# Input projection of a hybrid encoder layer: ten pairs of weight tiles as two-by-two block products in a stage of their own

## The chip, the cores and the metric

The kernel runs on one core of a Trainium2 chip. That core has five engines with instruction queues of their own: TensorE (PE in the profile; its weight loads are PEld), VectorE (DVE), ScalarE (ACT), GpSimd (POOL) and SyncE (SP), whose queue issues nearly all DMA transfers here. The metric is the device time of one launch in microseconds (us).

## The reference

One step of a one-layer encoder over 1152 tokens: 1024 of a prompt and 8 x 16 sample tokens with caches. In float32:

```python
h = rmsnorm(x, g_pre_mix)
qa, ka, va, qb, kb, vb, ga, gb = project(h, w_in)        # h @ w_in, 1024 -> 4352 columns
oa = band attention of qa over ka, va                    # 8 heads, 2 kv heads, own chunk + 2, sinks, T5 bias
ob = band attention of qb over kb, vb                    # 8 heads, own chunk + 8, relative bias
merged = sigmoid(ga) * (oa @ w_oa) + sigmoid(gb) * (ob @ w_ob)
x = x + rmsnorm(merged @ w_out, g_post_mix)
f, conv_new = conv_ffn(rmsnorm(x, g_pre_ffn), ...)       # up and gate, causal conv, gelu, down
x = x + rmsnorm(f, g_post_ffn)
```

Beside x it returns the last rows of ka, va, kb and vb and the state of the convolution.

## The kernel before

**Number format.** Each float32 operand of a large product is split into a high and a low part (`hi`, rounded to the type fp32r, and `lo`, the rest), and three matmuls (hi x hi, hi x lo, lo x hi) stand for one. `mm3` (L117 to L123) does this for the projections.

**Layout.** Activations lie transposed: channels on the 128 partitions, tokens along the rows. The 4352 columns of `w_in` are 34 tiles of 128. Tiles 0 to 3 are the queries of branch A (two heads each), 4 and 5 its keys and values, 6 to 9, 10 to 13 and 14 to 17 queries, keys and values of B, 18 to 33 the two gates.

**Stages.** (1) Nine blocks of 128 tokens are loaded, normalised, transposed on TensorE (L131) and split into `hT`, three groups of 384 tokens (L133, L134). (2) Projections and attention together. (3) Output projections `w_oa`, `w_ob` with the gates (L579 to L615). (4) `w_out`, norms, transposes (to L740). (5) The FFN's up and gate products (L774), with the convolution between. (6) The down product (L1039) and the final norm.

**Projections.** A tile's weights come in one transfer of 512 KB and are split by ACT (L105) and POOL (L108). Its product is three pieces, one for each group, of 24 matmuls of 128x384 into one PSUM bank (`piece`). ACT evacuates a piece: queries, keys and values into `raw` (L214), gates into `gt`, stored to `gate_dr` in DRAM (L276, L277). When a tile of queries, keys or values is complete, `q_done`, `k_done` or `v_done` split its rows, send new cache rows out and transpose values.

**Attention.** There are eight units: 0 to 3 for A (two heads each), 4 to 7 for B. A unit has six steps, four over 256 prompt tokens each and two over four samples each. A step computes scores (L344), adds bias and takes the minimum on DVE (L347), exponentiates on ACT (L352), scales (L367); the next step transposes the result on TensorE (L384, copied out at L386 and L388) and multiplies with the values (L399, L401), and the output goes to `o_dr` in DRAM (L402). Pieces of projection are laid between these items in quarters of six matmuls (`spread`): unit u carries the projections of unit u + 1 and `gates_per_unit` pieces of gates. Nine gate pieces remain after the last unit; one stands before its last transposes, one before its last `values`, seven behind.

**Stage 3's inputs.** The eight rows of `o_dr` are read into two buffers (`or`, pool `wx`, L588) and split (L589 on DVE, L590 on DVE or POOL) into `oT`. The first output tile needs units 0 to 3 for its first branch and 4 to 7 for its second.

**Bias tables.** Two small tables are replicated over 128 rows in DRAM by 16 transfers (L96); each unit reads its bias from them (L308, L414). This stands after the first two pieces of ka and va.

**Order.** The framework's scheduler orders each engine's instructions by the order of the program and by an estimate of when each is ready, so that a piece of projection may go ahead of a step that is not ready. On the chip each queue is then worked off in that order; waits are semaphores. Memory of a finished pool is given to the next pool at the same place, tile by tile.

**The block form.** Stages 5 and 6 already use a two-by-two block product with seven block products. In stage 5 the left factors are sums of quarters of two weight tiles, the right ones (b11, b21, t3, t2, t1, b22, t4) sums of quarters of the activations, each 512 channels by 576 tokens. A product (`product`, L770 to L775) is 24 matmuls of 128x288. `head_away` computes the two products that need only the first half of the activations and stores them, `tail` does the other five.

## Time and profile before

| | us |
|---|---|
| median of 3 runs | 1684.24 (1683.12 to 1687.8) |
| the profiled execution, its own time | 1683.2 |
| its span, from the first to the last instruction | 1681.1 |
| PE busy | 1631.1 |
| DVE busy | 964.7 |
| ACT busy | 668.7 |
| POOL busy | 315.1 |

A row of the profile names a line of the kernel, an engine, an operation and its tiles (written <- read, numbers left out in the page). `idle ... <- X` tells how long the engine stood still before these instructions and what released it. Matmuls are pipelined, so that the duration of one (0.34 us) is longer than the distance to the next (0.17 us). In windows, busy time counts each engine by itself. The profiled execution is one of several; its sums are compared with its own time.

### The profile page before, as it was taken

What the parts mean: (1) busy time and instruction counts of PE and PEld (TensorE: products, weight loads), DVE (VectorE), ACT (ScalarE), POOL (GpSimd) and SP (SyncE); (2) the same over time, 40 slices, a digit from 0 to 9 for tenths busy, and PEclk for the clock granted to TensorE, in tenths of its full rate; (3) what the DMA queues carried; (4) which work ended last, traced back from release to release, by engine and by line L of the source; (5) the groups of instructions that cost most, each with busy time, mean ns of one, the idle gap of its engine ahead of it and who ended that gap; (6) DMA issues with size and microseconds to landing.
All of it is one profiled execution on the core that took longest, in us unless ns stands there. A gap on an engine that the chain in (4) does not pass through costs nothing. (4 is left out here: it accounts for less than half of the span.)

```text
span 1681.1 us, 26782 instructions
## 1 busy us (share of the span) xinstructions
PE 1631.1 (97%) x10599; PEld 1505.6 (90%) x10599; DVE 964.7 (57%) x1815; ACT 668.7 (40%) x1309; POOL 315.1 (19%) x349
## 2 busy tenths in 40 slices
PE   5999999999999999999989899999999998999997
PEld 4999889899899999988889899999999997888886
DVE  6134442444443345444479676666666665965986
ACT  5244443333333322242354344444444444534342
POOL 2322122122221134420001211111111110000003
PEclk9999999999999999999999999999999999999999
DMA  5522323222222255452245322122212218043023
GB/s 190 177 87 80 110 82 95 71 70 69 77 85 70 70 174 178 137 179 100 85 134 159 111 82 79 68 76 80 72 62 79 80 55 315 36 182 138 1 90 136
DMA packets 84846, 177.37 MB, mean 106 GB/s; under 512 B 20536, under 2 KB 45672, under 8 KB 84720
## 3 DMA queue, kind: packets, MB, share of 16 engines
q1 hardware_dynamic: 84720, 175.65, 31.3%
q8 instruction: 83, 1.36, 0.4%
q14 instruction: 43, 0.35, 0.1%
HBM read 131.78 MB, written 48.56 MB: 107 GB/s over the span
## 5 line engine op out<-in xcount | busy, mean ns | idle before, releaser
L774 PE MATMUL x<-xot,s 128*128 128x288 f32 x1152 | 158.0, 295 | 1.8 <-DVE s L668 1.5
L774 PEld LDWEIGHTS x<-xot,s 128*128 128x128 f32 x1152 | 154.9, 188 | 2.2 <-DVE s L668 1.7
L1039 PE MATMUL x<-wbp,zap 128*128 128x512 f32 x576 | 135.3, 389 | 0.0
L1039 PEld LDWEIGHTS x<-wbp,zap 128*128 128x128 f32 x576 | 108.1, 188 | 22.4
L352 ACT ACTIVATE p<-p,m 128x256 f32<-128x256 f32 (+4 forms) x128 | 75.2, 589 | 105.3 <-DVE m L347 105.2
L1039 PE MATMUL p<-wbp,zap 128*128 128x512 f32 x432 | 102.0, 392 | 0.0
L667 ACT ACTIVATE s<-uw 128x512 fp32r<-128x512 f32 x96 | 60.0, 626 | 96.6 <-issue 43.2
L1039 PEld LDWEIGHTS p<-wbp,zap 128*128 128x128 f32 x432 | 82.0, 190 | 17.2
L870 DVE SCALAR_TENSOR_TENSOR wk<-w,cw,wk 128x128 f32<-128x128 f32 (+2 forms) x144 | 84.0, 619 | 7.8 <-ACT wk L868 7.0
L774 PE MATMUL x<-xob,s 128*128 128x288 f32 x576 | 82.6, 299 | 4.2 <-ACT wk L868 3.0
L668 DVE TENSOR_TENSOR s<-uw,s 128x512 fp32r<-128x512 f32 x96 | 67.3, 702 | 32.2 <-ACT s L667 32.2
L774 PEld LDWEIGHTS x<-xob,s 128*128 128x128 f32 x576 | 79.6, 191 | 4.7 <-ACT wk L868 3.2
L774 PE MATMUL z<-xot,s 128*128 128x288 f32 x576 | 80.7, 295 | 0.0
L774 PE MATMUL z<-xot,a 128*128 128x288 f32 x576 | 80.7, 295 | 0.0
L668 DVE TENSOR_TENSOR a<-uw,a 128x512 fp32r<-128x512 f32 x62 | 42.8, 691 | 63.5 <-ACT a L667 62.3
L774 PEld LDWEIGHTS z<-xot,s 128*128 128x128 f32 x576 | 78.1, 188 | 0.0
L774 PEld LDWEIGHTS z<-xot,a 128*128 128x128 f32 x576 | 78.1, 188 | 0.0
L774 PE MATMUL x<-xob,a 128*128 128x288 f32 x456 | 63.9, 295 | 0.0
L774 PE MATMUL y<-xob,a 128*128 128x288 f32 x456 | 63.9, 295 | 0.0
L774 PEld LDWEIGHTS x<-xob,a 128*128 128x128 f32 x456 | 61.8, 188 | 0.0
L774 PEld LDWEIGHTS y<-xob,a 128*128 128x128 f32 x456 | 61.8, 188 | 0.0
L347 DVE CUSTOM_DVE_ANT_0 p<-s,bt 128x320 f32<-128x320 f32 (+4 forms) x64 | 29.0, 489 | 56.2 <-PE s L344 55.5
(1216 smaller groups left out, 4123.0 us busy)
## 6 DMA issues: line engine op xcount, KB each, us to landing
uw<-in_w_upg SPq DMA_DIRECT2D x53, 512.0 KB, 4.4
gate_dr<-gt SPq DMA_DIRECT2D x48, 192.0 KB, 2.2
gg<-gate_dr SPq DMA_DIRECT2D x16, 576.0 KB, 3.9
z_dr<-wk SPq DMA_DIRECT2D x24, 256.0 KB, 2.1
z_dr<-wk SPq DMA_DIRECT2D x24, 224.0 KB, 1.9
xt<-in_x SPq DMA_DIRECT2D x9, 512.0 KB, 6.9
or<-o_dr SPq DMA_DIRECT2D x8, 576.0 KB, 4.3
xr<-in_x SPq DMA_DIRECT2D x9, 512.0 KB, 3.7
```

Source lines behind the costliest of these rows:

```text
L347: nc.vector.tensor_tensor_reduce(p[h][:, c * cw:(c + 1) * cw], ps[:, h, 0:cw], un.bt[h][:, w - n + c * cw:w - n + (c + 1) * cw], 1.0, leas ...
L352: nc.scalar.activation(p[h][:, 0:n], p[h][:, 0:n], AF.Exp, bias=least[h], scale=-1.0, accum_out=st.d[:, h, i:i + 1])
L667: nc.scalar.activation(sp[:, 0], src, AF.Copy)
L668: nc.vector.tensor_tensor(sp[:, 1], src, fr(sp[:, 0]), op=ALU.subtract)
L774: nc.tensor.matmul(ps[c], w[:, i, k], xo[name][:, j, c, k], start=first and k + i + j == 0, stop=last and k == 3 and i == 1, skip_group_ch ...
L870: nc.vector.scalar_tensor_tensor(out, src(t), cw[:, f, t:t + 1], out, op0=ALU.mult, op1=ALU.add)
L1039: nc.tensor.matmul(ps, z[:, i, k, c], w[:, j, k], start=first and n == 0, stop=last and n == 2, skip_group_check=True)
```

## The change

Twenty of the 34 tiles, as the ten pairs `pairs`, are computed in a stage ahead of attention, in the block form of stage 5; the other 14 stay as pieces between the attention steps. All 34 have their rows in DRAM (`in_dr`), and attention reads what it needs (`fetch`).

- The transposes now fill four quarters in float32 (`qa`, `qb`) by ACT; the splits (`parts_of`) run on 288 tokens at a time, the first two behind the third and the fifth block. The split activations are in `xk`, which takes the memory of `hT` and stays through attention.
- Five pairs go through `head_away`: two products, one part stored to `a1_dr`, one finished quarter to `in_dr`. Two of these stand ahead of the bias tables, three behind. Then each pair has its `tail`.
- `fetch(0)` stands before the first unit, `fetch(u + 1)` before the fourth step of unit u. It loads rows of 1152 tokens, scales queries on ACT, and goes on as `q_done`, `k_done`, `v_done` do.
- 42 pieces remain. `pieces_per_unit` lays 39 into the units, three remain after the last one.
- Memory for stages 3 to 6 (`r1`, `r2`) is opened only after attention. `left_factors`, `product` and `banks` now serve both block stages.

```diff
--- before
+++ after
+    in_dr = [dram.tile([P, T], F32, name=f"in_dr{i}") for i in range(34)]
+    gate_dr = in_dr[18:]
...
+    def left_factors(raw, ahead, name, part):
+        a11, a12, a21, a22 = raw[:, 0, 0:4], raw[:, 0, 4:8], raw[:, 1, 0:4], raw[:, 1, 4:8]
+        if not ahead:
+            yield part(a11, f"a11_{name}")
+            yield part(a12, f"a12_{name}")
+        nc.vector.tensor_tensor(a11, a11, a21, op=ALU.subtract)
+        yield part(a11, f"s3_{name}")
+        nc.vector.tensor_tensor(a11, a22, a11, op=ALU.subtract)
+        yield part(a11, f"s2_{name}")
+        nc.vector.tensor_tensor(a21, a21, a22, op=ALU.add)
+        yield part(a21, f"s1_{name}")
+        nc.vector.tensor_tensor(a12, a12, a11, op=ALU.subtract)
+        yield part(a12, f"s4_{name}")
+        yield part(a22, f"a22_{name}")
+
...
+    xkp = xk_stack.enter_context(tc.tile_pool(name="xk", bufs=1, reuse_waits="tile"))
+    xk = [xkp.tile([P, 2, 4, T], F32R, name=f"xk{i}") for i in range(2)]
...
+        pairs = [(4, 5), (0, 1), (2, 3), (10, 14)] + [(18 + n, 26 + n) for n in range(6)]
+        NA = 5
+        a1_dr = [dram.tile([P, 2, CW], F32, name=f"a1_dr{f}") for f in range(NA)]
+        rf = {}
...
+        def parts_of(t, src, c):
+
+            hi = t[:, 0, :, chunk(c)]
+            nc.scalar.activation(hi, src[:, :, chunk(c)], AF.Copy)
+            nc.vector.tensor_tensor(t[:, 1, :, chunk(c)], src[:, :, chunk(c)], fr(hi), op=ALU.subtract)
...
+        for i, name in enumerate(("b11", "b12")):
+            rf[name] = xk[0][:, :, :, i * 2 * CW:(i + 1) * 2 * CW]
+        for i, name in enumerate(("b21", "b22")):
+            rf[name] = xk[1][:, :, :, i * 2 * CW:(i + 1) * 2 * CW]
...
+        def head_away(f):
+
+            raw = wraws.pop(f, None) or weights(f, 1)
+            xb = banks(psx, f"ixh{f}")
+            product(xb, split_left(raw[:, 0, 0:4], f"ih11_{f}"), of(rf["b11"]), True, True)
+            a = copy_out(xb, two_chunks(f"iah{f}"))
+            nc.sync.dma_start(a1_dr[f][:], a[:])
+            yb = banks(psz, f"iyh{f}")
+            product(yb, split_left(raw[:, 0, 4:8], f"ih12_{f}"), of(rf["b21"]), True, True)
+            store(plus(yb, a, two_chunks(f"ich{f}")), pairs[f][0], 0)
...
-                sq = xp.tile([P, D], F32, name=f"sq{tb}", tag="sq", bufs=2)
+                if tb in (1, 3):
+                    wraws[tb // 2] = weights(tb // 2, 1)
                 st = xp.tile([P, 2], F32, name=f"st{tb}", tag="st")
-                nc.scalar.activation(sq[:], xt[:], AF.Square, accum_out=st[:, 0:1])
+                xn = xp.tile([P, D], F32, name=f"xn{tb}", tag="xn")
+                nc.scalar.activation(xn[:], xt[:], AF.Square, accum_out=st[:, 0:1])
                 rstd_of(st[:, 0:1], st[:, 1:2])
-                xn = xp.tile([P, D], F32, name=f"xn{tb}", tag="xn")
                 nc.vector.scalar_tensor_tensor(xn[:], xt[:], st[:, 1:2], gp[:], op0=ALU.mult, op1=ALU.mult)
-                transpose_to(pst, xn, hT, tb)
-                if tb in (2, 5):
-                    name = ("ka", "va")[tb // 3]
-                    early[name] = weight_tile(w_in[4 + tb // 3], name)
-
+                for q, quads in enumerate(((b11, b12), (b21, b22))):
+                    pt = psz.tile([P, 4, P], F32, name=f"tp{tb}_{q}", tag="ps")
+                    for k in range(4):
+                        nc.tensor.transpose(pt[:, k], xn[:, (4 * q + k) * P:(4 * q + k + 1) * P], ident[:])
+                    done = 0
+                    while done < P:
+                        h, t = divmod(tb * P + done, 2 * CW)
+                        n = min(P - done, 2 * CW - t)
+                        nc.scalar.activation(quads[h][:, :, t:t + n], pt[:, :, done:done + n], AF.Copy)
+                        done += n
+                if tb in (2, 4):
+                    for name, b in (("b11", b11), ("b21", b21)):
+                        parts_of(rf[name], b, tb // 2 - 1)
+
+            for f in range(2):
+                head_away(f)
+
...
+            replicate(tab_b, ext_b, eb, EXT_B)
...
+            replicate(tab_a, ext_a, ea, EXT_A)
+
+        tpool = [ph.enter_context(tc.tile_pool(name=f"t{i}", bufs=1, reuse_waits="tile")) for i in (3, 2, 1)]
...
+        def right_factors():
+
+            for n, pool in zip(("t3", "t2", "t1"), tpool):
+                rf[n] = pool.tile([P, 2, 4, 2 * CW], F32R, name=n)
+            for c in range(2):
+                cc = chunk(c)
+                parts_of(rf["b12"], b12, c)
+                nc.vector.tensor_tensor(b11[:, :, cc], b12[:, :, cc], b11[:, :, cc], op=ALU.subtract)
+                nc.vector.tensor_tensor(b12[:, :, cc], b22[:, :, cc], b12[:, :, cc], op=ALU.subtract)
+                parts_of(rf["t3"], b12, c)
+            yield
+            for c in range(2):
+                cc = chunk(c)
+                nc.vector.tensor_tensor(b12[:, :, cc], b22[:, :, cc], b11[:, :, cc], op=ALU.subtract)
+                parts_of(rf["t2"], b12, c)
+            yield
+            for c in range(2):
+                parts_of(rf["t1"], b11, c)
+            yield
+            for c in range(2):
+                cc = chunk(c)
+                parts_of(rf["b22"], b22, c)
+                nc.vector.tensor_tensor(b21[:, :, cc], b21[:, :, cc], b12[:, :, cc], op=ALU.subtract)
+            rf["t4"] = rqa.tile([P, 2, 4, 2 * CW], F32R, name="t4", tag="q")
+            for c in range(2):
+                parts_of(rf["t4"], b21, c)
+            yield
+
...
+        def head_back(f):
+            a = two_chunks(f"ia{f}")
+            nc.sync.dma_start(a[:], a1_dr[f][:])
+            return left_factors(weights(f), True, f"i{f}", split_left), banks(psx, f"ix{f}"), a
+
+        def tail(f, ops, xb, a, forms):
+            def take(name):
+                t = two_chunks(f"{name}{f}")
+                return copy_out(xb, t) if a is None else plus(xb, a, t)
+
+            t0, t1 = pairs[f]
+            zb = banks(psz, f"iz{f}")
+            product(zb, next(ops), of(rf["t3"]), True, False)
+            next(forms, None)
+            product(xb, next(ops), of(rf["t2"]), a is not None, False)
+            next(forms, None)
+            u2 = take("iu")
+            product(xb, next(ops), of(rf["t1"]), False, False)
+            next(forms, None)
+            u4 = take("iv")
+            store(plus(zb, u4), t1, 1)
+            product(xb, next(ops), of(rf["b22"]), False, True)
+            store(take("iw"), t0, 1)
+            product(zb, next(ops), of(rf["t4"]), False, True)
+            store(plus(zb, u2), t1, 0)
+
+        forms = right_factors()
+        for f in range(2, NA):
+            head_away(f)
+            if f == 2:
+                next(forms)
+        for f in range(len(pairs)):
+            tail(f, *(head_back(f) if f < NA else head(f)), forms)
...
+        def dense_pieces(col):
 
             box = {}
 
             def run(g):
                 if g == 0:
...
+                    box["w"] = weight_tile(w_in[col], f"w{col}")
+                w, c = box["w"], slice(g * GW, (g + 1) * GW)
+                ps = psd.tile([P, GW], F32, name=f"d{col}_{g}", tag="d")
+                for k in range(0, KD, 2):
+                    mm3(ps[:], w, [xk[k // 4][:, j, :, c] for j in range(2)], k % 4, 2, start=k == 0,
+                        stop=k == KD - 2, wk0=k)
+                    if k < KD - 2:
+                        yield
+                gt = gst.tile([P, GW], F32, name=f"gt{col}_{g}", tag="gt")
+                nc.scalar.activation(gt[:], ps[:], AF.Copy)
+                nc.sync.dma_start(in_dr[col][:, c], gt[:])
...
+        def rows(col, name, done, scale=None):
+
+            raw = rawp.tile([P, T], F32, name=f"{name}raw", tag="raw")
+            nc.sync.dma_start(raw[:], in_dr[col][:])
+            if scale is not None:
+                nc.scalar.activation(raw[:], raw[:], AF.Copy, scale=scale)
+            done(raw)
...
+        def fetch(u):
+
             un = units[u]
             if u < 4:
-                out = []
                 if u == 0:
-                    out += projection_pieces(4, "ka", 1.0, k_done(shared_a, "a", ka_new, 896))
-                    out += projection_pieces(5, "va", 1.0, v_done(shared_a, "a", va_new, 896))
-                return out + projection_pieces(u, f"q{u}", -0.125, q_done(un, u))
-            p = u - 4
-            return (projection_pieces(10 + p, f"k{u}", 1.0, k_done(un, f"{u}", kb_new[p], 512))
-                    + projection_pieces(14 + p, f"v{u}", 1.0, v_done(un, f"{u}", vb_new[p], 512))
-                    + projection_pieces(6 + p, f"q{u}", -0.125, q_done(un, u)))
+                    rows(4, "ka", k_done(shared_a, "a", ka_new, 896))
+                rows(u, f"q{u}", q_done(un, u), -0.125)
+                if u == 0:
+                    rows(5, "va", v_done(shared_a, "a", va_new, 896))
+            else:
+                p = u - 4
+                rows(10 + p, f"k{u}", k_done(un, f"{u}", kb_new[p], 512))
+                rows(6 + p, f"q{u}", q_done(un, u), -0.125)
+                rows(14 + p, f"v{u}", v_done(un, f"{u}", vb_new[p], 512))
...
+        dense_tiles = [6, 11, 15, 7, 12, 16, 8, 13, 17, 9, 24, 32, 25, 33]
+        pieces = []
+        for col in dense_tiles:
+            pieces += dense_pieces(col)
...
-        first = unit_pieces(0)
-        for g in range(NG):
-            run(first[g], first[NG + g])
-            if g == 0:
-                bias_tables()
-        run(*first[2 * NG:])
-        gates_per_unit = [6, 6, 3, 3, 3, 3, 3, 12]
+        fetch(0)
+        pieces_per_unit = [4, 4, 4, 4, 6, 6, 6, 5]
...
         for u in range(8):
-            dense = unit_pieces(u + 1) if u < 7 else []
-            n = gates_per_unit[u]
-            lead = 3 if u < 3 else 0
-            dense = gates[:lead] + dense + gates[lead:n]
-            gates = gates[n:]
+            n = pieces_per_unit[u]
+            dense, pieces = pieces[:n], pieces[n:]
...
+                if i == 3 and u < 7:
+                    fetch(u + 1)
...
-        run(gates[0])
+        run(pieces[0])
         for _ in transposes(prev):
             pass
-        run(gates[1])
+        run(pieces[1])
         values(prev)
-        run(*gates[2:])
+        run(*pieces[2:])
+    xk_stack.close()
+    r1 = [r1_stack.enter_context(tc.tile_pool(name=f"r1{i}", bufs=1, reuse_waits="tile")) for i in range(4)]
+    r2 = r2_stack.enter_context(tc.tile_pool(name="r2", bufs=2, reuse_waits="tile"))
```

192 lines of the change are left out of this document (89 added, 103 removed).

## The prediction

> **What bounds the kernel now.** I read the page first, then what TensorE waited for over the whole span, then windows around the stages the change touches.
>
> ```profile
> span 1681.1 us, 26782 instructions
> PE 1631.1 (97%) x10599; PEld 1505.6 (90%) x10599; DVE 964.7 (57%) x1815; ACT 668.7 (40%) x1309; POOL 315.1 (19%) x349
> ```
>
> TensorE is the bound. The answer on its waits adds up to less than 40 us, and almost all of them stand at the beginning of a stage:
>
> ```profile
> PE tp L131 <- DVE xn L157: 7.7, 1, 7.7
> PE tp L131 <- DVE hT0l L134: 7.5, 2, 6.1
> PE p20s L1039 <- ACT wbp L977: 4.9, 1, 4.9
> PE x L774 <- ACT wk L868: 3.0, 1, 3.0
> PE r L725 <- ACT wt L105: 2.7, 1, 2.7
> PE mp L607 <- ACT gt L276: 2.7, 1, 2.7
> PE xh L774 <- ACT h L667: 2.5, 1, 2.5
> PE x L774 <- DVE s L668: 1.5, 1, 1.5
> ```
>
> So a change pays by what it takes off TensorE, and loses by every new place where TensorE runs dry. Three windows show how full it is (columns: length, then busy time and count of PE, PEld, DVE, ACT, POOL, then clock and DMA): projections with attention from 41.6 to 602.9 us, one unit of branch A, one unit of branch B.
>
> ```profile
> 41.60:602.90 561.30, 561.30 (x4047) 508.30 (x4046) 216.26 (x779) 211.88 (x559) 122.42 (x110) 1.00 0.29 88
> 101.70:155.20 53.50, 53.50 (x401) 48.26 (x396) 21.30 (x88) 22.53 (x69) 11.14 (x11) 1.00 0.30 90
> 404.40:480.90 76.50, 76.50 (x565) 68.88 (x561) 32.95 (x106) 28.34 (x67) 17.37 (x16) 1.00 0.25 76
> ```
>
> TensorE never pauses there: attention is a chain of small steps on four engines, and the projections of 34 weight tiles, cut into 102 pieces of 24 matmuls, fill every hole in it. The change takes 60 of these 102 pieces away.
>
> **The saving on TensorE.** What counts is the distance between starts. The first two rows are 18 matmuls apart in a projection of today (128x384); the last two are neighbouring products in the FFN stage, which already works in the form that the change brings (24 matmuls of 128x288 each).
>
> ```profile
> 607.16 0.34 PE L121 MATMUL g14p<-hT0h,g14s 128*128 128x384 f32 x1
> ...
> 610.28 0.34 PE L121 MATMUL g14p<-hT0h,g14s 128*128 128x384 f32 x1
> ...
> 1108.02 3.36 PE L774 MATMUL z<-xot,a 128*128 128x288 f32 x24
> 1111.21 3.36 PE L774 MATMUL x<-xob,a 128*128 128x288 f32 x24
> ```
>
> 3.12 us / 18 = 0.1733 us for 384 columns; 3.19 us / 24 = 0.133 us for 288. A pair of tiles costs 144 x 0.1733 = 24.96 us today and seven products of 3.20 us, 22.4 us, then: 2.56 us less, and **25.6 us** for ten pairs. The two prices are nearly proportional to the columns (288/384 of 0.1733 is 0.130), so the eighth that the algebra leaves out really comes off.
>
> The Trainium skill, "TensorE: Matmul & The Clock Gate", section on the back-to-back issue gap, says otherwise: in a stream that loads weights for each matmul, about 81 ns at 128 columns and 131 ns at 512. An estimate on the straight line between them gives 114 ns at 384 and 102 ns at 288, so that a pair would go from 16.4 to 17.1 us and the change would lose 7 us on TensorE instead of gaining. The rows above do not agree with it.
>
> **Vector work of the new stage.** Per pair the FFN form has five to seven splits of a left factor on ACT and DVE, four sums on DVE and the reading of the banks. In the FFN stage this runs beside the convolution without a hole in TensorE, with 0.133 us pitch, so behind 22.4 us of products I cost it at nothing; without that cover it would be the splits alone, some 7 x 0.7 us a pair. The stores to DRAM lie beside the products too.
>
> **The start.** Columns from here: start, duration, engine, line, operation; the ACT rows are groups (count, busy, mean in ns).
>
> ```profile
> 41.60 0.45 PE L121 MATMUL kap<-hT1h,kas 128*128 128x384 f32 x1
> L154 ACT ACTIVATE sq<-xt 128x1024 f32<-128x1024 f32 x9 | 9.5, 1055 | 5.1 <-DMA xt<-in_x 4.8 <-DVE xn L157 0.3
> L133 ACT ACTIVATE hT1h<-tp 128x512 fp32r<-128x512 f32 x6 | 3.6, 599 | 4.1 <-PE tp L131 3.9
> L630 ACT ACTIVATE xot<-bq 128x1152 fp32r<-128x1152 f32 x8 | 9.2, 1159 | 0.9 <-DVE bq L917 0.9
> 43.45 5.57 SPq L96 DMA_DIRECT2D ext_b<-tab_b  x8
> 49.06 8.56 SPq L96 DMA_DIRECT2D ext_a<-tab_a  x8
> ```
>
> Today TensorE works without a break from 41.6 us, having done two pieces (8.3 us) and the transposes: 33.3 us are lost. In the changed kernel no product can be finished before five blocks of tokens are normalised, transposed and split, because its right side is 576 columns wide (today's first piece needs three). ACT sets the pace: nine squares (1.06 us), eighteen copies (0.60) and four splits of 1152 elements (1.16) are 25 us, behind a first square at 4.3 us and a wait of 2.3 for the second block, so all is in place at 32 to 34 us. What products of the two first pairs slip in before that is gain; I take 4 us of them and 34 us, a loss of 30, so **-3 us**. If all four first products (12.8 us) slip in it is -12. If none do, and the 14.1 us that SP spends on issuing the bias tables delay the third pair's weights, which stand behind it on SP's queue, it is +8.
>
> **The ramp of the new stage.** After the five half-finished heads (ten products, 32 us) the tails need t3, t2, t1, b22 and t4, made by DVE in about that time. The FFN stage has the same ramp: its waits for splits are the 2.5 and 1.5 us quoted above, its waits for the convolution (L868) have no counterpart. So **+4 us**; 0 if DVE keeps up, 12 if the convolution's waits stand for others.
>
> **From the new stage into attention.** A new wait: the rows of ka, va and q0 come back from DRAM into memory that t3, t2 and t1 leave. The pair with ka and va is the first one finished, and the weights of the next dense tile can be there, so little is late. Stages begin with 2.7 us (L725, L607) to 4.9 us (L1039) today: **+2.7**, between 0 and 4.9.
>
> **Attention with less filler.** A unit of A holds nine pieces today: 53.5 - 9 x 4.16 = 16.1 us are its own. With four it takes 32.7 us, or 5.5 us for each of six steps. A unit of B holds twelve: 26.6 us its own, with six pieces 51.6, or 8.6 us a step. The chain that a step's transposes wait for, from the first DVE reading of the last scores to the last scaling, in A and in B:
>
> ```profile
> 205.71 0.48 DVE L347 CUSTOM_DVE_ANT_0 p<-s,bt,sinkb 128x256 f32<-128x256 f32 x1 [2.11 <-PE s L344]
> ...
> 208.15 1.14 DVE L367 TENSOR_SCALAR p<-p,dn 128x256 f32<-128x256 f32 x4
> ...
> 487.30 0.49 DVE L347 CUSTOM_DVE_ANT_0 p<-s,bt 128x320 f32<-128x320 f32 x1 [3.80 <-PE s L344]
> ...
> 490.70 1.94 DVE L367 TENSOR_SCALAR p<-p,dn 128x640 f32<-128x640 f32 x4
> ```
>
> 3.6 us of 5.5 and 5.3 us of 8.6; DVE, with 21.3 and 33.0 us a unit, would be busy 65% and 64%. Steps overlap by one, so I price new waits at only **+2 us**. The upper end is the rival below, 16 us; a gain is excluded, since nothing waits now. The same price holds the row fetches, which put a load and behind it a store that waits for this load on SP, ahead of the next sample caches and bias rows: half a unit of time stands before them.
>
> **The end of attention: the dear one.** The output projections (L607 to L609) need all eight units read back from DRAM and split, through two buffers that take the place of the last `values`.
>
> ```profile
> 600.57 2.38 PE L399 MATMUL o<-pk,vs 128*64 128x256 f32 x24
> 632.46 0.34 PE L123 MATMUL g15p<-hT2h,g15s 128*128 128x384 f32 x1
> 635.47 0.44 PE L607 MATMUL mp<-oT,wo0s 128*128 128x384 f32 x1 [2.67 <-ACT gt L276]
> 637.13 0.52 PE L608 MATMUL mp<-oT,wo0s 128*128 128x384 f32 x1
> 736.82 0.34 PE L609 MATMUL mp<-oT,wo7s 128*128 128x384 f32 x1
> L588 SPq DMA_DIRECT2D or<-o_dr x8: 319/320/417, 604.2 to 632.6; - x8
> L589 DVE CAST oT<-or x8: 759/760/2325, 608.3 to 638.4; 128x1152 fp32r<-128x1152 f32 x8
> L590 DVE TENSOR_TENSOR oT<-or,oT x5: 1359/1359/3720, 612.0 to 639.2; 128x1152 fp32r<-128x1152 f32 x5
> L590 POOL TENSOR_TENSOR oT<-or,oT x3: 2647/3060/3199, 611.3 to 635.3; 128x1152 fp32r<-128x1152 f32 x3
> DMA to landing us min/median/max: 3.8/4.3/5.3
> ```
>
> Today the chain runs from 602.9 to 640.6 us (last split 639.2 + 1.36), 37.7 us, and seven gate pieces (29.1 us) hide it. The change leaves one piece there. Without their stores the chain is shorter: one buffer takes four rounds of 4.3 + 0.76 us and two splits on POOL (3.06) and two on DVE (1.36), 29.1 us, and the first load is issued 1.3 us after the values: 30.4 us. By then TensorE can have done 45 of the 576 matmuls (the first branch of one weight tile, 36, and three of the four k of one group). The other 531 take 92.0 us, and 1.5 us go to the slow matmuls after a wait (next paragraph): 123.9 us from the values to the last of them. Today it is 133.9, less six pieces (25.0) 108.9. So **+15 us**. It is 8.8 if the next weight tile's first branch runs early too (36 matmuls, 6.2 us), and 22.3 if the chain keeps its 37.7 us.
>
> After the wait of 3.0 us at 632.5 the matmuls stand 0.32 us apart for ten matmuls (the row at 637.13 is one): 1.5 us. The Trainium skill (same page, the HAM clock gate) calls this half rate after an idle window of about 3.4 us; the trace agrees in kind. If the long wait at this place fell into two such idles, the sum below would be 1.5 us higher.
>
> **The sum.** -25.6 - 3 + 4 + 2.7 + 2 + 15 = **-4.9 us** on the profiled execution's own 1683.2 us (its span 1681.1 and 2.1 around it): 1678.3 us. That execution is 1.0 us under the median of 1684.24.
>
> **The rivals.** *The holes are hidden* (chance 0.22): four first products slip in early, DVE keeps up with the ramp, the end costs 8.8: -25.6 - 12 + 0 + 0 + 2 + 8.8 = -26.8, 1656; half way there from my sum is 1667. For it: FFN's steady 0.133. Against: memory for the read-back is free only after the values.
>
> *Gain and hole cancel* (0.20): the read-back keeps its 37.7 us, 22.3 instead of 15, with the rest as in the sum: +2.4, 1685.6. For it: 3.8 us is the shortest landing seen, and the two buffers stay.
>
> *Attention waits for its softmax* (0.20, slower): in steps of A with the smaller shares, two or three of a unit's 16 quanta (1.04 us each), TensorE has between last scores and transposes the previous values (1.1), the next scores (0.35) and 1.5 us of dense work, 3.0 us against a chain of 3.6 and its signals, some 1 us short. Sixteen such steps, if the order is kept strictly, are 16 us instead of 2: 1692.3. It decides from about 10 us of such waits on. Against it: later pieces may be moved ahead.
>
> *The cost per matmul is mostly fixed* (0.03, slower): if 288 columns cost only 10% less than 384 here, a pair would take 168 x 0.156 = 26.2 us, 1.2 more than today: 12 us up instead of 25.6 down, 1716. The pitch rows speak against it. It is the direction of the page quoted above.
>
> **How the numbers follow.** My forecast has 0.35. What a measurement of this kernel tells from no change is 0.3%, 5.1 us around 1684.2. The forecast, at -5.9 against that median, lies just beyond, and I put 0.25 of its 0.35 to faster, 0.09 to same and 0.01 to slower; the hidden holes are faster, the cancelling case 0.13 same and 0.07 slower, the two others slower: faster 0.47, same 0.22, slower 0.31. The range goes from a good half of the hidden-hole case, 1661, to beyond the softmax case with a slow start, 1698; the forecast's own is 1671 to 1685.
>
> **What would show it.** Right: 42 pieces of 0.173 us pitch, ten pairs of 22.4 us, a hole of 15 us or more ahead of L607's successor whose release is the cast or split of `oT`, and windows in attention that are still full. Wrong: waits of `pt` or `o` for DVE spread over the A units (softmax), a first product before 25 us or after 40 (start), a gap below 8 us ahead of the output projections (the end).

## The result, and the profile after

The changed kernel takes **1702.52 us** (median of 4 runs, 1701.11 to 1705.01) beside 1684.01 for the kernel before on the same chip: a ratio of 1.0107, 95% interval 1.0088 to 1.0127. It is slower by some 18 us, where 6 us faster was forecast. The profiled execution took 1702.66 us, with this head of its page:

```profile
span 1700.9 us, 27746 instructions
PE 1622.1 (95%) x10839; PEld 1488.6 (88%) x10839; DVE 1102.4 (65%) x2021; ACT 707.2 (42%) x1375; POOL 266.7 (16%) x329
```

TensorE is busy 9 us less than before, and the span is 19.8 us longer: the work came off, and idle time came in. The windows say where. Columns: stretch, length, then busy time and count of PE, PEld, DVE, ACT, POOL, then granted clock, DMA share, GB/s. First the kernel before: up to the first full stream of projections, projections with attention, output projections.

```profile
0.00:41.60 41.60, 23.74 (x122) 19.49 (x122) 26.79 (x43) 24.26 (x41) 11.06 (x21) 1.00 0.53 192
41.60:632.60 591.00, 590.77 (x4214) 537.33 (x4213) 233.35 (x791) 219.12 (x569) 133.92 (x114) 1.00 0.31 95
632.60:737.00 104.40, 101.72 (x578) 101.37 (x576) 48.04 (x80) 28.89 (x38) 43.26 (x31) 0.98 0.47 146
```

Then the changed kernel: start, product stage, attention with 42 pieces, output projections.

```profile
0.00:45.70 45.70, 27.37 (x168) 24.77 (x168) 31.05 (x41) 34.57 (x58) 5.72 (x15) 0.96 0.66 225
45.70:261.30 215.60, 213.02 (x1588) 211.88 (x1587) 128.67 (x212) 67.27 (x121) 7.18 (x8) 0.99 0.40 140
261.30:635.00 373.70, 358.79 (x2823) 299.90 (x2821) 224.12 (x777) 176.51 (x494) 75.59 (x91) 0.98 0.40 125
635.00:754.50 119.50, 106.85 (x577) 103.63 (x576) 61.16 (x90) 32.31 (x41) 50.17 (x33) 0.91 0.48 158
```

Taken off these lengths are the pieces at their full pace (4.16 us each) and the products at theirs (0.1333 us). The rest is what each stage costs beyond them:

| | before | after | difference | forecast |
|---|---|---|---|---|
| ten pairs: 60 pieces, or 1680 products | 249.6 | 224.0 | -25.6 | -25.6 |
| start, and ramp of the new stage | 41.6 - 2 x 4.16 = 33.3 | 261.3 - 224.0 = 37.3 | +4.0 | +1 |
| attention | 591.0 - 100 x 4.16 = 175 | 373.7 - 42 x 4.16 = 199 | **+24** | +4.7 |
| last piece to last output projection | 104.4 | 119.5 | +15.1 | +15 |
| all later stages | 944.1 | 946.4 | +2.3 | 0 |

These sum to +19.8. The pace of the products is as expected: 72 of them in 9.56 us from the first of these rows (TensorE's timeline) to the last, 0.1328 us each.

```profile
200.80 3.35 PE L142 MATMUL iz<-t,s_i 128*128 128x288 f32 x24
203.99 6.53 PE L142 MATMUL ix<-t,s_i 128*128 128x288 f32 x48
210.36 3.35 PE L142 MATMUL ix<-xk,s_i 128*128 128x288 f32 x24
```

Three rows of what TensorE waited for, over the whole span (us in total, times, longest):

```profile
PE vta L457 <- DMA varaw<-in_dr: 7.8, 1, 7.8
PE mp L775 <- POOL oT L757: 6.8, 2, 4.8
...
PE pt L571 <- DVE p L554: 3.1, 2, 1.6
```

The waits `mp` for `oT` are the hole at the end, foreseen with its place and releaser. The wait of 7.8 us for the v rows at the entry of attention was not, and the waits `pt` for `p` are too small to make the rest of the 24 us. In attention the trace has two kinds of loss: gaps, measured here from the start of the last matmul before to the start of the next, and stretches at half the clock, half of which is lost. The entry has a gap of 8.3 us and 6.8 us of half clock, 11.7 in all; three stalls at 311, 409 and 463 us have gaps of 1.8, 1.9 and 1.9 and two stretches of 3.4 us behind them, 9.0 in all. Some 3 us lie in smaller gaps. Four readings follow.

**The entry.** SP's queue, then GpSimd's, then TensorE:

```profile
257.41 0.33 SPq L108 DMA_DIRECT2D w15r<-in_w_in  x1
...
264.62 0.33 SPq L108 DMA_DIRECT2D w7r<-in_w_in  x1
...
265.84 0.33 SPq L418 DMA_DIRECT2D varaw<-in_dr  x1
```

```profile
262.24 2.36 POOL L104 TENSOR_TENSOR w11s<-w11r,w11s 128x1024 fp32r<-128x1024 f32 x1
```

```profile
271.24 1.12 PE L457 MATMUL vta<-ident,varaw 128*128 128x128 f32 x4 [7.82 <-DMA varaw<-in_dr]
```

SP issues nothing in the last six of the 7.2 us between the first two of these loads: at its head stands the load of `w7r`, whose buffer GpSimd frees with the split of `w11` (262.24 + 2.36 = 264.60). The load of the v rows stands behind it, and in TensorE's order the transposes of v stand ahead of pieces that could run. The wait costs twice. Windows in which half the clock was granted (the second and third lie behind the stalls at 409 and 463 us, the last at the end):

```profile
267.50:274.30 6.80, 3.06 (x13) 2.97 (x14) 0.69 (x1) 0.80 (x2) 0.00 (x0) 0.50 0.77 276
410.90:414.30 3.40, 3.40 (x12) 2.91 (x13) 1.86 (x9) 1.36 (x5) 0.36 (x2) 0.50 0.62 144
465.50:468.90 3.40, 3.40 (x17) 2.87 (x17) 0.80 (x2) 1.53 (x5) 1.95 (x4) 0.50 0.77 232
639.60:660.10 20.50, 11.88 (x31) 9.16 (x32) 11.61 (x10) 3.61 (x3) 4.93 (x2) 0.50 0.78 276
```

**VectorE beside GpSimd: the stall at 409 us.** VectorE's timeline ahead of the stall at 409 us, GpSimd's beside it, and the stall:

```profile
404.20 0.43 DVE L428 CAST k5h<-k5raw 128x512 fp32r<-128x512 f32 x1 [1.27 <-PE s L531]
404.55 0.48 DVE L534 CUSTOM_DVE_ANT_0 p<-s,bt,sinkb 128x256 f32<-128x256 f32 x1
...
405.36 1.00 DVE L428 CAST k5h<-k5raw 128x512 fp32r<-128x512 f32 x1
406.28 1.85 DVE L428 CAST q5h<-q5raw 128x512 fp32r<-128x512 f32 x2
408.05 1.23 DVE L549 TENSOR_TENSOR dn<-dn,se 128x4 f32<-128x4 f32 x1
...
409.78 1.71 DVE L554 TENSOR_SCALAR p<-p,dn 128x256 f32<-128x256 f32 x4
```

```profile
404.78 1.30 POOL L429 TENSOR_TENSOR k5l<-k5raw,k5h 128x512 fp32r<-128x512 f32 x1 [0.44 <-DVE k5h L428]
406.44 1.41 POOL L429 TENSOR_TENSOR k5l<-k5raw,k5h 128x512 fp32r<-128x512 f32 x1 [0.36 <-DVE k5h L428]
407.80 2.67 POOL L429 TENSOR_TENSOR q5l<-q5raw,q5h 128x512 fp32r<-128x512 f32 x2
```

```profile
410.86 1.33 PE L571 MATMUL pt<-ident,p 128*128 128x128 f32 x4 [1.64 <-DVE p L554]
```

The same cast takes 0.43 us ahead of GpSimd's subtractions and 1.00 beside them; a sum of four elements a row takes 1.23 us. From the reading of the scores (404.55) to the end of the scaling lie 6.9 us, where the kernel before needed 3.6: three of the four casts of the rows read back stand between, and GpSimd stretches them. The Trainium skill, "SBUF — State Buffer", section "Who interferes with whom", gives the rule: VectorE and GpSimd share one pair of ports, as an exclusive lock held for the whole instruction; casts and `tensor_scalar` can take both ports, and a `tensor_tensor` with two inputs in SBUF (the memory on the chip in which tiles lie) contends with GpSimd's reads. These rows agree; the reading of scores out of PSUM, 0.48 us, is not stretched.

**Rows that land late: the stalls at 311 and 463 us.** VectorE ahead of the first; then SP, ScalarE, VectorE and TensorE at the second:

```profile
307.90 0.43 DVE L428 CAST k4h<-k4raw 128x512 fp32r<-128x512 f32 x1 [2.05 <-DMA k4raw<-in_dr]
```

```profile
457.22 0.33 SPq L108 DMA_DIRECT2D w24r<-in_w_in  x1
457.66 0.37 SPq L418 DMA_DIRECT2D q6raw<-in_dr  x1
```

```profile
462.42 1.16 ACT L420 ACTIVATE q6raw<-q6raw 128x1152 f32<-128x1152 f32 x1 [2.66 <-DMA q6raw<-in_dr]
```

```profile
463.61 0.43 DVE L428 CAST q6h<-q6raw 128x512 fp32r<-128x512 f32 x1 [1.51 <-ACT q6raw L420]
464.07 0.42 DVE L588 COPY oo<-o 128x256 f32<-128x256 f32 x1
```

```profile
464.55 0.65 PE L571 MATMUL pt<-ident,p 128*128 128x128 f32 x4 [1.68 <-DVE oo L588]
```

Here VectorE stands still: a cast waits for rows read back, and the reading of scores (311) or the copy `oo` (463), on which TensorE depends, stands behind it; at 311 GpSimd also stretches the second cast, to 0.90 us. The load of the q rows comes to SP's head only at 457.66 us, behind a weight load that waited 3.1 us for GpSimd's split of `w17`, as at the entry; the load of the k rows waited 1.8 us for a row buffer that GpSimd still read.

**The end.** The eight read-backs (starts from 631.7 to 657.3 us), GpSimd's share of their splits, and TensorE behind the last piece:

```profile
L755 SPq DMA_DIRECT2D or<-o_dr x8: 319/320/372, 631.7 to 657.3; - x8
L757 POOL TENSOR_TENSOR oT<-or,oT x3: 2621/2684/3118, 638.8 to 661.0; 128x1152 fp32r<-128x1152 f32 x3
```

```profile
636.78 0.41 PE L774 MATMUL mp<-oT,wo0s 128*128 128x384 f32 x1 [1.62 <-DVE oT L756]
641.97 0.69 PE L775 MATMUL mp<-oT,wo0s 128*128 128x384 f32 x1 [4.77 <-POOL oT L757]
```

From the end of the last values at 630.75 us to the last output projection at 754.5 lie 123.8 us; the forecast had 123.9.

### The profile page after: what moved, and what is told of

Read it like the earlier page. It is cut to its first block, busy times and chain, and to the rows that moved or that the text cites. A ratio compares the mean times of both kernels' runs of the same rounds, so it can differ in the third digit from the quotient of the medians.

```text
span 1700.9 us, 27746 instructions
## 1 busy us (share of the span) xinstructions
PE 1622.1 (95%) x10839; PEld 1488.6 (88%) x10839; DVE 1102.4 (65%) x2021; ACT 707.2 (42%) x1375; POOL 266.7 (16%) x329
## 5 line engine op out<-in xcount | busy, mean ns | idle before, releaser
L142 PE MATMUL ix<-t,s_i 128*128 128x288 f32 x480 | 65.3, 295 | 0.0
L571 PE MATMUL pt<-ident,p 128*128 128x128 f32 x360 | 58.9, 287 | 6.2 <-DVE p L554 3.1
L142 PEld LDWEIGHTS ix<-t,s_i 128*128 128x128 f32 x480 | 64.2, 188 | 0.0
## 6 DMA issues: line engine op xcount, KB each, us to landing
z_dr<-wk SPq DMA_DIRECT2D x24, 224.0 KB, 1.9
```

The costliest lines, as they stand in the source:

```text
L142: nc.tensor.matmul(ps[c], w[:, i, k], right(j, c, k), start=first and k + i + j == 0, stop=last and k == 3 and i == 1, skip_group_check=True)
L571: nc.tensor.transpose(pt[:, h * nb + b], st.p[i][h][:, c:c + P], ident[:])
```

## The experiments

"Attention" and "end" in the tables are worked out as above: from the first to the last piece, less 4.16 us for each of them, and from there to the last output projection. Each ratio is to runs of the kernel before on the same chip. Their medians lie between 1683.2 and 1685.4 us, so a difference of 2 us or less between two rows says little.

### Is attention short of filler?

Four pairs instead of ten, so that 78 pieces are left (69 of them beside attention, 9 behind it); and the opposite, all 42 pieces ahead of attention.

```diff
-pairs = [(4, 5), (0, 1), (2, 3), (10, 14)] + [(18 + n, 26 + n) for n in range(6)]
+pairs = [(4, 5), (0, 1), (2, 3), (10, 14)]
...
-pieces_per_unit = [4, 4, 4, 4, 6, 6, 6, 5]
+pieces_per_unit = [8, 8, 8, 8, 10, 10, 10, 7]
```

> Edit of the changed kernel: only the four pairs of queries, keys and values stay in the new stage; the six pairs of gates are dense pieces again, 78 instead of 42 (8 for each unit of A, 10 of B, 7 for the last, 9 behind it). Rows still pass through DRAM as in the changed kernel. Theory (less filler opens the holes): products 15.4 us dearer, the end 13 to 15 us and the waits in attention 15 to 19 us cheaper, so 1683 to 1690. Rival (rows fetched through DRAM hold the steps up): only the end is cheaper, 1700 to 1705.

```diff
+run(*pieces)
+pieces = []
 fetch(0)
-pieces_per_unit = [4, 4, 4, 4, 6, 6, 6, 5]
+pieces_per_unit = [0] * 8
...
```

> Edit of the changed kernel: all 42 dense pieces run ahead of attention, none is left between its steps. Theory (attention needs more than the 42 pieces, 175 us, to be filled): the eight units alone last about as long as with the pieces, 330 us or more, and the kernel some 150 us longer or more, 1850 and up. Rival (attention alone is short, what waits is elsewhere): the units last 180 to 220 us, the kernel 1710 to 1750.

| | us | ratio to before | attention | end |
|---|---|---|---|---|
| before | | | 175 | 104.4 |
| changed kernel | 1702.5 | 1.0107 | 199.0 | 119.5 |
| four pairs | 1704.1 (1697.0 to 1708.8) | 1.0119 [1.0085, 1.0152] | 198.1 | 104.0 |
| no pieces beside attention | 1792.0 (one run) | | 283.7 | |

With nearly twice the filler attention costs the same 198 us, so thin filler does not make the 24 us. The same is left, the rows read back, and its waits show it (waits of TensorE in attention; then a row of VectorE's timeline):

```profile
PE o L586 <- DVE pk L573: 6.8, 2, 4.5
PE vta L457 <- DMA varaw<-in_dr: 4.3, 1, 4.3
```

```profile
479.44 5.95 DVE L554 TENSOR_SCALAR p<-p,dn 128x640 f32<-128x640 f32 x4
```

Four scalings of 640 columns take 5.95 us there, beside GpSimd's splits of the q rows and of a weight tile; in the kernel before the four of a step took 1.94. A copy that TensorE needs stands behind them. The other 15 us come back as forecast: with nine pieces behind attention the end takes 104.0 again. But the saving is then only 10.2 us (672 products, 89.6 us, for 24 pieces, 99.8), and start and ramp cost 44.7 instead of 37.3. Alone, attention is 284 us long:

```profile
444.30:728.00 283.70, 243.68 (x1806) 153.73 (x1805) 209.87 (x772) 143.40 (x439) 38.79 (x61) 0.84 0.33 100
```

Beside 39 pieces (162 us) the changed kernel needs 199 + 162 = 361. So attention still hides about half of the time of the pieces moved into it; neither limit in the expectation was met.

### What does the entry cost?

Four attempts to have the v rows earlier. First, the splits of the two weight tiles that GpSimd holds at the entry go to VectorE:

```diff
-box["w"] = weight_tile(w_in[col], f"w{col}")
+box["w"] = weight_tile(w_in[col], f"w{col}", lo_engine="vector" if col in (6, 11) else "gpsimd")
```

> Edit of the changed kernel: the low parts of the first two dense weight tiles (6 and 11) are made by DVE instead of POOL. Theory (the 7.8 us wait for the rows of va at the entry to attention comes from SP's queue: the load of va stands behind a weight load that waits for POOL): POOL is free 5 us earlier, the wait falls to 3 us or less and the slow clock behind it goes, 6 to 10 us less than the changed kernel. Rival (the rows themselves come late through DRAM): the wait stays, within 2 us of 1702.

Then free buffers for the v rows of the first unit, so that no row buffer is waited for: two buffers of the probabilities, loaded through SP, the same through ScalarE, and finally buffers of `stk`.

```diff
-rows(5, "va", v_done(shared_a, "a", va_new, 896))
+va = [pp.tile([P, 640], F32, name=f"varaw{i}", tag="p", bufs=8) for i in range(2)]
+nc.sync.dma_start(va[0][:], in_dr[5][:, 0:640])       # second run: nc.scalar
+nc.sync.dma_start(va[1][:, 0:512], in_dr[5][:, 640:T])
+v_done(shared_a, "a", va_new, 896)(va)
...
```

> The v rows of the first unit are loaded into two buffers of the probabilities, which are free then, and need not wait for a row buffer that GpSimd holds. Theory (the entry costs what its wait shows, 8.3 us, and 3.4 for the 6.8 us at half clock behind it): 8 to 12 us less, 1690 to 1695. Rival (the first units are paced by the softmax, so that a shorter entry comes back as longer stalls in the units behind it, as with the faster split of the weight tile): within 4 of 1702.5.

> As the run with the v rows of the first unit in free buffers, but their two loads are issued from ScalarE's queue instead of SP's, where a weight load that waits for its slot stood ahead of them (SP issued nothing from 256.9 to 263.4 us). Theory (the entry costs its wait of 6 to 8 us and 3.4 of half clock): wait under 1 us, 8 to 11 us less than 1702.5, 1691 to 1695. Rival (a shorter entry comes back as longer stalls behind it): within 4 of the 1701 of that run.

```diff
+va = [stk.tile([P, SEQ], F32, name="varaw0", tag="vs", bufs=2),
+      stk.tile([P, SEQ], F32, name="varaw1", tag="k")]
+nc.sync.dma_start(va[0][:], in_dr[5][:, 0:SEQ])
+nc.sync.dma_start(va[1][:, 0:P], in_dr[5][:, SEQ:T])
...
```

> The v rows of the first unit are loaded into a free buffer of the transposed values and one of the k rows, so that their two loads stand ahead of the weight load w15r in SP's queue. Nothing else is changed. Theory (the entry costs its wait, 8.3 us, and 3.4 us of half clock): the wait is under 1 us and 8 to 11 us are saved, 1691 to 1695. Rival (the first units are paced by their softmax, and the stalls behind grow as the entry shrinks): within 4 of 1702.5.

| | us | ratio to before | gap at the entry | half clock behind it | attention |
|---|---|---|---|---|---|
| changed kernel | 1702.5 | 1.0107 | 8.3 | 6.8 | 199.0 |
| tiles 6 and 11 by VectorE | 1702.3 | 1.0108 [1.0093, 1.0123] | 5.6 | 6.8 | 200.0 |
| other buffers, SP | 1701.0 | 1.0093 [1.0078, 1.0108] | 6.2 | 6.8 | 198.2 |
| other buffers, ScalarE | 1705.5 | 1.0122 [1.0106, 1.0139] | 8.0 | 13.7 | 201.5 |
| `stk` buffers, SP | 1692.8 | 1.0051 [1.0034, 1.0067] | none | 0 | 190.1 |

The first three did not test what they were meant to: a long wait stayed. In the first it fell from 7.8 to 5.3 us, but behind the stall at 311 us came 6.8 us at half clock that the changed kernel does not have, and the time stayed. In the second the loads still came behind `w7r` on SP (267.9 us), in the third behind a scaling of the next unit's q rows, for which ScalarE waited 12.7 us. Another buffer or queue does not help as long as something waiting stands ahead. The last run changes that order (SP's timeline):

```profile
254.23 0.33 SPq L487 DMA_DIRECT2D varaw<-in_dr  x1
254.61 0.42 SPq L488 DMA_DIRECT2D varaw<-in_dr  x1
...
257.61 1.03 SPq L108 DMA_DIRECT2D w15r<-in_w_in  x1
```

The wait is gone and the time falls by 9.7 us, of the 11.7 that gap and half clock promised (8.3, and half of 6.8). The stalls at 300, 400 and 454 us are still there, 1.9 us each: the entry is a loss of its own and does not come back behind.

### What do the row splits cost?

Three edits of the read-back: the rows of a unit spread over three steps; the same with each split at the end of its step, behind the normalisation; and the low parts computed by VectorE, without moving anything.

```diff
-if i == 3 and u < 7:
-    fetch(u + 1)
+fetch_step(u, i)    # k loaded at step 1, q at 2, v at 3; each split at the start of the next step
...
```

> The rows of a unit are read back and split over three steps of the unit before (k, then q, then v, each loaded one step ahead of its use) instead of all at one point, and the v rows of the first unit are used one step later. Theory (attention's 24 us beyond the forecast are the read-back itself: the wait at its entry with the half clock behind it, 11.5, and the bursts of row splits in VectorE's queue between a step's scores and its normalisation, three stalls of 1.8 to 2.0 with half clocks of 3.4 behind two of them, about 9): 12 to 20 us less, 1683 to 1691. Rival (the stalls move to another step because the softmax is short of cover there anyway): within 4 of 1702.5.

```diff
 values(prev) if prev.kind == "p" else sample_values(prev)
+use_step(u, i)      # loads as above; k, q, v split at the end of steps 2, 3, 4
...
```

> The rows are loaded at the start of steps 1, 2 and 3 of a unit and split at the end of steps 2, 3 and 4, behind the step's normalisation, instead of all at the start of step 3, ahead of its scores. Theory (the place of the splits in VectorE's queue, between scores and normalisation, makes the stalls): 6 to 12 us less, 1690 to 1697. Rival (the softmax of these steps is short of cover with or without the splits): within 3 of the spread kernel's 1699.7.

```diff
-nc.gpsimd.tensor_tensor(lo[:, c], raw[:, c], fr(hi[:, c]), op=ALU.subtract)
+nc.vector.tensor_tensor(lo[:, c], raw[:, c], fr(hi[:, c]), op=ALU.subtract)
```

> The low parts of the q and k rows (L429, 1.3 to 1.5 us on GpSimd) are computed by VectorE instead of GpSimd, at the same place. Theory (in attention the trace of the changed kernel has VectorE instructions that take 1.0 to 1.8 us instead of 0.15 to 0.55 whenever they run beside a subtraction of GpSimd, 25.5 us in all, and these stretch the steps whose softmax TensorE waits for): the stretched ones fall below 12 us, the stalls at 311, 409 and 463 us go with their half clocks, 6 to 11 us less, 1691 to 1697. Rival (VectorE's own time for the subtractions takes their place): within 3 of 1702.5.

| | us | ratio to before | attention |
|---|---|---|---|
| spread, split ahead of the scores | 1699.7 | 1.0091 [1.0075, 1.0106] | 198.0 |
| spread, split behind the normalisation | 1695.1 | 1.0057 [1.0041, 1.0073] | 192.9 |
| low parts by VectorE | 1694.7 | 1.0065 [1.0041, 1.0088] | 191.8 |

Spreading alone does next to nothing, and my theory of bursts fell with it: how many rows come at once matters little here. The gains of the other two cannot be read off the changed kernel. Both spread kernels also use the first v rows a step later, which leaves waits of 6.6 and 6.3 us at the entry instead of 7.8, so the place of the splits is worth the difference between them, 4.6 us. In its trace only the q casts moved behind the scaling; the k casts still stand between (403.29 and 404.44 us), one of them stretched to 1.00 us, and the way from scores to scaled rows takes 4.9 us instead of 6.9. Of the 7.8 us of the last run some 2.4 lie at the entry, where GpSimd is free earlier and the waits sum to 5.4 us.

With the low parts on VectorE the stretching is gone (VectorE's timeline at the same place as above):

```profile
402.25 0.42 DVE L428 CAST k5h<-k5raw 128x512 fp32r<-128x512 f32 x1
402.59 0.42 DVE L428 CAST q5h<-q5raw 128x512 fp32r<-128x512 f32 x1
402.93 0.15 DVE L549 TENSOR_TENSOR dn<-dn,se 128x4 f32<-128x4 f32 x1
```

0.42 instead of 1.00 us and 0.15 instead of 1.23, the way from scores (400.84) to scaled rows takes 3.9 us, and the stall at 409 us is not there. The wait at 311 us falls from 1.5 to 0.7 us; that at 463 us stays, 1.9 us with its half clock, so the expectation that all three go failed there. Three of the four subtractions stand behind the normalisation in that order too, and one cast fewer between, so this run does not part the port from the place entirely.

### What fills the end?

The pool of the read-back buffers opened ahead of the pool of the split outputs; two weight tiles of additional projections behind the last values; four of the 42 pieces moved there.

```diff
+wx = ph.enter_context(tc.tile_pool(name="wx", bufs=2, reuse_waits="tile"))
 op = ph.enter_context(tc.tile_pool(name="op", bufs=1, reuse_waits="tile"))
...
-wx = ph.enter_context(tc.tile_pool(name="wx", bufs=2, reuse_waits="tile"))
```

> Edit of the changed kernel: the two read-back buffers of stage 3 (pool wx) are opened ahead of oT instead of behind it, so that they take memory that is free before the last values. Theory (the end is held by the read-back chain, and that by memory that comes free late): two or three of the eight units are read and split under attention, the first output product waits less, 8 to 12 us less than the changed kernel, 1691 to 1695. Rival (the pace of landing and splits sets it wherever it starts, or the slow clock does): within 3 us of 1702.

```diff
 run(*pieces[2:])
+for col in (34, 35):          # weights of tiles 0 and 1, into spare rows
+    run(*dense_pieces(col))
...
```

> Adds two weight tiles of projections (6 pieces, 144 matmuls, 25.0 us at 173.3 ns), written to spare rows that nobody reads, behind the last values. Theory (the 15 us lost at the end are a hole behind the last values that these matmuls would fill): it costs 5 to 13 us, 1707 to 1716, and the half clock at the end is gone. Rival (the end is bound by the queue of loads, which starts only when the last of the work is through): the hole stays behind the added pieces, 1724 to 1730.

```diff
-pieces_per_unit = [4, 4, 4, 4, 6, 6, 6, 5]
+pieces_per_unit = [5, 5, 5, 4, 5, 5, 4, 2]
```

> The same 42 pieces of projections, but 7 instead of 3 of them behind the last step of attention (5,5,5,4,5,5,4,2 beside the units instead of 4,4,4,4,6,6,6,5). Theory (attention has filler to spare: it hides some 110 to 130 us and has 162): the end loses 10 to 15 us, attention gains under 5, 1690 to 1697. Rival (the units that give their pieces away become bound by their softmax): attention gains as much as the end loses, 1699 to 1708.

| | us | ratio to before | attention | end |
|---|---|---|---|---|
| changed kernel | 1702.5 | 1.0107 | 199.0 | 119.5 |
| read-back pool first | 1698.9 | 1.0089 [1.0074, 1.0104] | 200.5 | 115.0 |
| 25.0 us of work added | 1711.8 | 1.0158 [1.0143, 1.0173] | 200.5 | 107.3 |
| 7 pieces behind | 1700.6 | 1.0096 [1.0081, 1.0111] | 211.9 | 107.7 |

Opening the pool first brings 3.6 us, between theory and rival: the read-backs start at 552.5 us instead of 631.7, but the first split only at 633.3 instead of 635.9. 25.0 us of matmuls cost 9.3: the other 15.7 are the hole. The windows of that run show the added pieces without a gap and the output projections behind them near their old length; the half clock there falls from 20.5 to 6.8 us:

```profile
635.00:660.80 25.80, 25.54 (x148) 25.22 (x147) 16.03 (x11) 7.27 (x10) 10.97 (x4) 1.00 0.71 233
660.80:768.00 107.20, 103.27 (x577) 102.36 (x575) 46.49 (x80) 28.74 (x38) 43.16 (x31) 0.97 0.42 141
```

So the end is a hole that pieces would fill, but the changed kernel has none to spare: moved from attention, they win 12 us at the end and lose 13 before it. The new stalls stand in the first three units, which got more pieces, and in the sixth, which got fewer; why the first three stall more with five pieces than with four was not settled.

### Do the losses add?

First, spread rows, read-back pool first and 7 pieces behind. Then low parts by VectorE, splits behind the normalisation, first v rows through ScalarE, read-back pool first; the same with 6 pieces behind the last step (units 6 and 7 get 5 and 3); and the same with the v rows in the `stk` buffers.

> Rows spread over three steps, 7 pieces behind the last step, and the pool of the read-back buffers opened ahead of the pool of the split outputs. Theory (the read-back and the end are separate losses and add up): 12 to 20 and 10 to 15 less, 1669 to 1682, under the kernel before. Rival (what is freed in one place opens in another): 1690 or more.

> Together: rows split by VectorE alone and behind the normalisation, first v rows from ScalarE's queue, and the read-back pool opened first at the end. Theory (separate losses that add: 7.8, some 4 for the place, 8 to 11 for the entry, 3.6 for the end): 1675 to 1684. Rival (they fill the same holes): 1688 to 1694.

> As e13, with 6 instead of 3 pieces behind the last step (units 6 and 7 get 5 and 3 instead of 6 and 5) and the last two tiles of rows exchanged in order. Theory (the hole at the end is what is left, and attention has cover to spare now): 5 to 9 us less than e13. Rival (units 6 and 7 lose what the end wins, as in the run with 7 pieces behind): within 3 of e13.

> The same early load on top of: rows split by VectorE alone and behind the normalisation, read-back pool opened first, 6 pieces behind the last step. Theory (entry 4.8 us and 3.4 of half clock go): 1674 to 1679, faster than the kernel before. Rival (they come back): within 3 of 1684.

| | us | ratio to before | attention | end |
|---|---|---|---|---|
| spread, pool first, 7 behind | 1696.4 | 1.0061 [1.0044, 1.0078] | 203.7 | 108.4 |
| splits repaired, pool first | 1688.2 | 1.0028 [1.0015, 1.0042] | 190.6 | 114.6 |
| and 6 pieces behind | 1684.2 | 0.9993 [0.9980, 1.0005] | 194.5 | 106.9 |
| and v rows early | **1678.9** | **0.9969 [0.9957, 0.9981]** | 191.9 | 106.7 |

The first combination fell to its rival. In the second the wait for the v rows was still 4.2 us, behind the next unit's q rows on ScalarE; its 1688.2 lies at the edge of the rival, and its attention (190.6) is little below that with the low parts on VectorE alone (191.8). The third gained 4.0 us on it, between theory and rival; the last came out as its theory has it. So the losses add only in part: singly the gains are 9.7, 7.8, 4.6 and 3.6 us, 25.7 without the moved pieces, together with them 23.6. The last version beats both kernels, by 0.3% and 1.4%. Its windows, attention and output projections, and its read-backs, which now start at 545 us (their splits at 611):

```profile
260.50:627.20 366.70, 358.96 (x2824) 302.38 (x2823) 233.71 (x812) 179.57 (x497) 49.34 (x65) 0.98 0.43 136
627.20:733.90 106.70, 103.21 (x577) 102.25 (x576) 54.73 (x84) 28.75 (x38) 45.49 (x31) 0.97 0.44 145
```

```profile
L787 SPq DMA_DIRECT2D or<-o_dr x8: 319/320/429, 545.4 to 634.7; - x8
```

Attention still costs 17 us more than in the kernel before. Four gaps of 1.4 to 2.7 us (8.3 in all) and four half-clock stretches of 3.4 (half of them lost, 6.8) account for 15 of these. The trace names what stands behind them. At 454 and 509 us VectorE's cast of the q rows, with the copy `oo` behind it, waits 1.8 and 1.9 us for ScalarE's scaling, which waits 2.5 and 2.6 us for the rows; their load again follows a weight load on SP. At 306 us the cast of the k rows has waited 2.1 us for its rows. At 264 us the transposes of v wait 2.4 us for VectorE's last sums of the product stage (L186), which now stand behind the low parts of k and q. No run was aimed at these.

## Why the prediction was wrong

**The products: right.** -25.6 forecast and measured, because the price came from products of the same shape in this kernel. The rival in which the cost per matmul is mostly fixed is out.

**Start and ramp:** +1 forecast, +4.0 measured, inside the bounds given. The counts in the windows part them: by 45.7 us the 168 matmuls are 72 transposes and 96 of products (12.8 us), so the start loses 32.9 us where it lost 33.3, -0.4 instead of -3; the rest of the stage loses 215.6 - 1584 x 0.1333 = 4.4, with +4 forecast. The first product begins at 18.3 us, before the 25 us named as a sign of error, but half of it waits for further blocks until 30.6 us.

**The entry, priced at +2.7 with 4.9 as the upper end: wrong.** It cost 11.7 by the trace and 9.7 by the run without it. The step that failed is "so little is late". It took the longest wait at the start of a stage of today as the bound, though none of those stages begins with rows that GpSimd has to pass on, and it did not follow the load through SP's queue, where a weight load that waits for GpSimd now stands ahead. It also left out the half clock behind a wait, which it had priced at the end.

**Attention, priced at +2: wrong, by about 10 us.** The failed step is "the same price holds the row fetches". It looked at the fetch as loads on SP and took half a unit of time for enough. Two of the three stalls show rows that land late all the same, because their load waits for GpSimd, behind a weight load or for a row buffer. And each fetch also issues casts to VectorE and subtractions to GpSimd, all at one place ahead of a step's scores, where the kernel before split one row at a time when its projection was done. The prediction counted VectorE's busy time of a unit (65%) as room, not the order in its queue, and had no price for an engine that slows another. Against this, the softmax rival (16 us for sixteen short steps) named the right symptom, `pt` waiting for `p`, at only 3.1 us in two waits, and its mechanism is not what makes the 24 us: twice the filler changed nothing.

**The end: right,** +15 forecast and 15.1 measured, with releaser and place. *Gain and hole cancel* put 22.3 there, *the holes are hidden* 8.8; neither happened. That the figure fits so closely is luck, for the parts of its sum were off and offset each other: the last split ended 34.9 us behind the values instead of 30.4, but 64 of the 576 matmuls were started by then instead of 45, and the other 512 ran at 0.1733 us.

So the sum missed 24 us: entry 9, the rows in attention 10, start 3, later stages 2. The runs show 9.7 us for the entry. Of the 10 they show about half: 4.6 us for the place of the splits, some 5 for the low parts on VectorE, and little more for both at once. The other half stays without a run that shows its cause; the traces put most of it in the rows that land late. Both come from one omission: the new way of the rows through DRAM was priced as a transfer and not by the queues that its instructions enter. Mended as far as the runs go, with the read-back pool opened first and six pieces moved behind the last step, the kernel takes 1678.9 us. That this is the forecast's figure is chance, since other terms were moved too.

## What to carry to other kernels

Price a hand-over through memory by every instruction that it issues, on each in-order queue, by what stands ahead of its load there, and by what stands behind the one that waits; that time seems to be left says little. Look at the place of a new vector instruction between a chain's first and last step, and at what GpSimd does meanwhile, before trusting a share of busy time. A hole at the end of a stage can be filled only with work that was not hiding something else.

## What the runs showed of the hardware

VectorE's casts, scalings and sums of two operands in SBUF, started beside a subtraction of GpSimd, last until that is over: 0.43 to 1.00 us, 0.15 to 1.23. The forecast did not expect a loss from an engine that is busy 16% of the span.

TensorE's clock falls to half in stretches of 3.4 us and multiples of it (3.4, 6.8, 20.5 in the windows above), some 2 to 4 us after a wait began, and gaps of 1.9 us (waits of 1.6 and 1.7) are enough at 409 and 463 us. So such a gap costs up to 3.6. Its length alone does not decide: in the run with `stk` buffers a wait of 1.7 us that ends at 455.7 us has the full clock behind it, in the last version one of 1.1 us that ends at 305.9 us has half the clock behind it, from 307.8 to 311.2 us. The Trainium skill, "TensorE: Matmul & The Clock Gate", "What's actually happening", has the activity window of about 3.4 us; the lengths here agree. It puts the half rate after an idle window of that length; the waits here are shorter.

A load that is issued through another engine's queue does not leave the queueing: the v rows moved from SP to ScalarE came at 273.1 us instead of 265.8, behind an instruction that waited there.
